# Attention's value product with its operands swapped, in a two-block transformer on one core

## The chip, the core and the metric

The kernel runs on one core of a Trainium2 chip. The metric is device time in microseconds for one execution of the whole program; three runs of the kernel before are shown below. Engines are named as in the profile: PE is TensorE (PEld its weight loads), DVE is VectorE, ACT is ScalarE, POOL is GpSimd, SP issues the transfers.

## What is computed

The reference takes 256 tokens of width 1024 through two layers of a first block (a gated feed-forward, a mixer of four kinds of attention, a second feed-forward) and one layer of a second block (a pooling mixer and two kinds of attention, gated and merged). All of it is float32. What matters here is the last step of each attention, the softmax weights times the values, row by row of queries:

```python
p = jax.nn.softmax(logits, axis=-1)
o = jnp.einsum('bhqk,bkhd->bqhd', p, v)      # 64 values wide for each head
```

The differential attention of the first block has two softmax maps per head, subtracted before the product with the values. The other kinds (neighbourhood, latent, grouped query; in the second block sliding window and one they call MoBA) have one map per head.

## The kernel before, in words

Activations stand by token: two token tiles of 128 rows. Projections are matmuls with 512 moving columns; each weight and each activation is held as a pair (hi, lo) of float32r numbers, so that one product is three matmuls into `mmps`. Weights come by transfers on SP's queue, 512 KB each, through a stage of three buffers. ScalarE makes the `hi` part and VectorE (every third one GpSimd) subtracts it to get `lo` (class `Weights`, lines 159 to 227); six places (`N_SPLIT`) hold the pairs.

Attention runs in the background of these projections. It is written as generators; after each group of matmuls `tick` (line 449) resumes up to four steps that are due. When a step is due is decided while the program is laid down, by the class `Clock` (from line 62) with estimated times for every operation. Only the order of issue rests on these estimates; what waits for what follows from the data. An operation of ScalarE or VectorE that reads PSUM is laid down with a priority that lets it pass 14 others (`AHEAD`, line 153).

`softmax_pv` (line 575) is the pipeline of one attention. A job is one token tile and two heads (`ns = 2`), or one differential head with its two maps (`ns = 1`). It has four steps: `scores` (line 584) computes the scores and the softmax weights `E` by query; `transposes` (line 631) transposes `E` on TensorE and has ScalarE copy it to `PT`, by key; `values` (line 641) multiplies; `finish` (line 660) puts the result, divided by the softmax sums, into `y` by query. The loop from line 674 chooses among the steps by `e_at`, `p_at` and `y_at`, the times at which `timed` (line 417) found a step's last operation off TensorE to end.

In `values` the values `v`, 128 keys by 64, are the stationary operand, and `PT`, 128 keys by 128 queries, is the moving one. The result is by value feature: 64 partitions for each head, the second head in the upper half. ScalarE copies it to `yt`; `finish` transposes that back on TensorE (line 338) and VectorE multiplies by `rs`. Two differential jobs fill the halves of one `yt` and share one transpose.

In the second block the first token tile sees one key tile (`nk = 1`), the second sees two; in the first block all jobs see two. The first block has 8 differential jobs and 12 two-head jobs in each of its two layers; the second block has 16 two-head jobs. The names in the trace: `PT` with `v`, `ug`, `vm` or `vs` are value products, `sps` are score tiles, `tps` is the ring of two PSUM tiles (`psT`, line 319) that transposes and value products share. Small fp32 matmuls stand in the trace as two matmuls each.

Of the kernel before, what the change touches and what calls it, by code (L numbers as in the profile page):

```python
# [10 lines left out]
F = mybir.dt.float32  # L11
R = mybir.dt.float32r
ACTF = mybir.ActivationFunctionType
ALU = mybir.AluOpType
# [47 lines left out]
class Clock:  # L62
    """Estimated times of the engines while the program is laid down. Only the order of issue
    rests on them; the waits themselves come from the data."""

# [34 lines left out]
    def ring(self, tag, bufs, ap):  # L100
        """A new tile of a ring takes the place of the one `bufs` before it."""
        r = self.rings.setdefault(tag, [])
        r.append(ap.tensor.name)
        if len(r) > bufs:
            old = r[-1 - bufs]
            t = max((e[2] for b in (self.writes, self.reads) for e in b.pop(old, ())),
                    default=0.0)
            self._note(self.reads, ap, t, "dma")
# [17 lines left out]
class Engine:  # L126
    """Passes calls on and keeps the engine's estimated time; what frees PSUM goes first."""

# [30 lines left out]
class Weights:  # L159
    """Weights in the order of their use: DRAM -> fp32 stage -> exact (hi, lo) float32r pair.  # L160
    Past the first units, which are waited for, GpSimd does every third subtraction."""

# [9 lines left out]
    def add(self, ap, k, n, per, cols=None):  # L172
        """ap [k*128, n] in DRAM, cut into units of `per` row tiles."""
        v = ap.rearrange("(k p) n -> p k n", p=128)
        if cols is not None:
            v = v[:, :, cols[0]:cols[1]]
            n = cols[1] - cols[0]
        k0 = 0
        for m in per if isinstance(per, list) else [per] * (k // per):
            assert m * n <= self.UNIT  # L180
            self.units.append((v[:, k0:k0 + m, :], m, n))
            k0 += m
        assert k0 == k
# [31 lines left out]
    def can_cut(self):  # L215
        """Whether the next unit's place is free of reads yet to be laid down."""
        n = len(self.cut_at)
        return bool(self.units or self.staged) and all(
            i in self.ended for i in range(max(0, n - N_SPLIT), n - N_SPLIT + 1))

    def get(self):
        """(index, hi, lo) of the next unit."""
        while not self.ready:
            self.cut()
        self.got += 1
        return (self.got - 1,) + self.ready.pop(0)
# [6 lines left out]
def decoder(ctx, tc, a, out):  # L233
# [4 lines left out]
    PSUM = bass.MemoryType.PSUM  # L238
# [26 lines left out]

# [1 line left out]
    for l in range(L):  # L267
# [32 lines left out]

# [1 line left out]
    def v3(ap, n):  # L302
# [39 lines left out]
    def acc(pss, xh, xl, w, j, first, last):  # L342
        """pss += x^T w with x = xh + xl, w = wh + wl; xl wl lies under float32's last bit."""
        _, wh, wl = w
        for ps, c0, n in pss:
            mm(ps, xh, wh[:, j, c0:c0 + n], first, False)
            mm(ps, xh, wl[:, j, c0:c0 + n], False, False)
        for ps, c0, n in pss:
            mm(ps, xl, wh[:, j, c0:c0 + n], False, last)

    def rpow(ss, n, inv, tag):
        """(ss * inv + eps) ** -0.5; several columns by a bitwise start and Newton steps."""
        m = stat.tile([128, n], F, tag=f"m{tag}{n}", name="ms")
        dve.tensor_scalar(m, ss, inv, EPS, op0=ALU.mult, op1=ALU.add)
        r = stat.tile([128, n], F, tag=f"r{tag}{n}", name="r")
        if n < 4:
            gps.tensor_tensor(out=r, in0=m, in1=mhalf[:, :n], op=ALU.pow)
            return r
        I = mybir.dt.int32
        dve.tensor_scalar(r.bitcast(I), m.bitcast(I), -0.5, float(0x5f3759df), op0=ALU.mult,  # L360
                          op1=ALU.add)
        q = stat.tile([128, 16], F, tag="q", name="q", bufs=1)[:, :n]
        for _ in range(3):
            dve.scalar_tensor_tensor(out=q, in0=m, scalar=-0.5, in1=r, op0=ALU.mult,
                                     op1=ALU.mult)
            dve.tensor_tensor(out=q, in0=q, in1=r, op=ALU.mult)
            dve.scalar_tensor_tensor(out=r, in0=q, scalar=1.5, in1=r, op0=ALU.add, op1=ALU.mult)
        return r
# [28 lines left out]
    def trans_split(hi, lo, src, scale=None):  # L397
        """src [128, 128 m] transposed and split into hi, lo [128, m, 128]."""
        ps = psT()
# [17 lines left out]
    def timed(f, *args):  # L417
        """f's result, and the time at which the last of its ops ends."""
        before, clock.last = clock.last, 0.0
# [36 lines left out]
    def drain_until(cond):  # L456
        """Background steps alone until cond holds; a step that is not due is brought forward."""
        while not cond():
# [9 lines left out]
    class Norm:  # L468
        """Residual update of one token tile, then the next projection's operand: x^T times the
        gains, which stand by feature in `gain`; the token's factor comes with the results."""  # L470

# [27 lines left out]
    def proj(K, n, per, evac, skew=False):  # L499
        """[256, 128 K] x [.., n <= 512]; evac(t, ps) takes each token tile's result."""  # L500
        ps = [psM() for _ in range(2)]
# [22 lines left out]
    def wide(order, hi, lo, blocks, evac, before=None):  # L524
        """[256, 128 len(order)] x [.., 1024]. A block of row tiles is done for token tile 0,
        then for token tile 1."""
        nk = len(order)
# [43 lines left out]

# [1 line left out]
    att = {"busy": False, "pt": 0}  # L573

    def softmax_pv(jobs, post, scored=None, have_v=lambda: True):
        """jobs: dict(t, nk, qk=[(lhsT, rhs)] * 2, bias=[ap] * 2 or None, v=[[ap] * nk] * 2, y).
        Two score tiles per job: two heads, or with `nlam` the two maps of a differential head;
        two such jobs share one value tile. Software pipeline: scores, transposes, values, out."""
        n = len(jobs)
        diff = "nlam" in jobs[0]  # L580
        ns = 1 if diff else 2
        E, PT, YT, yts = {}, {}, {}, {}

# [56 lines left out]

        def values(i):
            jb = jobs[i]
            ps = psT()[:, :128]
            for s in range(ns):
                r = slice(64 * s, 64 * s + 64)
                for k in range(jb["nk"]):
                    mm(ps[r, :], jb["v"][s][k], PT[i][:, s, k, :], k == 0, k == jb["nk"] - 1)
            if diff and i % 2 == 0:
                yts[0] = wk.tile([128, 128], F, tag="yt", name="yt")
            elif not diff:  # L650
                yts[0] = wk.tile([128, 128], F, tag="yt", name="yt")
            yt = YT[i] = yts[0]
            if diff:
                r = slice(64 * (i % 2), 64 * (i % 2) + 64)
                copy(0, yt[r, :], ps[0:64, :])
            else:
                copy(0, yt, ps)
            del PT[i]

        def finish(i):  # L660
            if diff and i % 2 == 0:
                return
            ps = psT()[:, :128]
            T(ps, YT[i])
            if diff:
                for j in (i - 1, i):
                    dve.tensor_scalar(jobs[j]["y"], ps[:, 64 * (j % 2):64 * (j % 2) + 64],
                                      jobs[j]["rs"][:, 0:1], None, op0=ALU.mult)
            else:
                dve.tensor_tensor(out=jobs[i]["y"], in0=heads(ps),  # L670
                                  in1=jobs[i]["rs"][:, :, None].to_broadcast([128, 2, 64]),
                                  op=ALU.mult)
# [42 lines left out]
    def mixers(l, cols, rows, nlam, norm_out):  # L715
# [76 lines left out]
        def qk_transposed(u, new, colq, colk, scale, hd, free=None):  # L792
            """Head norms and transposes of q (256) and k (256), split; both gains go on q."""
            qcol = stat.tile([128, 1], F, tag="qcol", name="qcol")
# [285 lines left out]

    # ================= block 1 =================
    gains = const.tile([128, 9, 8], F, name="gains")
# [41 lines left out]

    # ================= block 2 =================
    one = pool("one", 1)
# [28 lines left out]

    # MoBA: one block of 256 keys, so the selected slots are all masked
    def ev_cq(t, ps):
# [69 lines left out]
    def pooling():  # L1227
        """Windowed means less x, as a product with a constant band over the tokens."""
        pT = [v3(gates[1][:, t, 512:1024], 128) for t in range(2)]
# [215 lines left out]
```

## Time and profile before

| what | value |
|---|---|
| median of three runs | 1353.05 us (1350.02, 1353.05, 1357.2) |
| profiled execution, first to last instruction | 1349.9 us |
| instructions in the trace | 17823 |
| mean granted TensorE clock | 0.986 |
| moved by transfers | 221.80 MB, mean 164 GB/s |

The three runs are times of whole executions. The profile is of one execution, of which the span alone is given. A busy engine in the table of the page is one that has an instruction under way; matmuls are pipelined, so the distance between the starts of two of them says more of their price than the duration of one.

### The profile page before, as it was taken

How to read it: one execution, taken by the hardware profiler on the slowest of the kernel's cores; microseconds unless marked ns; L12 is line 12 of the kernel's file. 1: busy time of each engine (PE TensorE's matmuls, PEld its weight loads, DVE VectorE, ACT ScalarE, POOL GpSimd, SP SyncE). 2: the span in 40 equal slices, each digit the busy share in tenths (PEclk: the TensorE clock that was granted, in tenths of full speed). 3: DMA queues.
4: the chain of work that ended last, by engine and by line, in shares of the span. 5: the costliest groups of instructions: out<-in, count | busy, mean ns of one | idle time of the engine just before them, and what ended most of it. 6: DMA issues, size and time to landing. Idle time of an engine off the chain costs nothing.

```text
span 1349.9 us, 17823 instructions
## 1 busy us (share of the span) xinstructions
PE 1305.5 (97%) x6514; PEld 1055.0 (78%) x6514; DVE 700.6 (52%) x1488; ACT 722.9 (54%) x1223; POOL 330.8 (25%) x171
## 2 busy tenths in 40 slices
PE   8999999989999999999999998999999999999997
PEld 7788888766788888788888876788888776678876
DVE  5534338886543433644325798563442544544365
ACT  6544346756644443544435676665443456656543
POOL 0022223211222222322222321132222231122221
PEclk9999999989999999999999899999999999999999
DMA  8766547332466655566555633156656572345652
GB/s 273 213 187 188 176 149 235 112 102 64 134 203 177 197 174 170 179 203 189 179 186 166 202 108 97 45 184 193 185 184 187 174 225 80 103 130 168 212 160 78
DMA packets 109815, 221.80 MB, mean 164 GB/s; under 512 B 7456, under 2 KB 30368, under 8 KB 109728
## 3 DMA queue, kind: packets, MB, share of 16 engines
q1 hardware_dynamic: 109152, 220.04, 53.8%
q8 instruction: 51, 0.84, 0.3%
q10 hardware_dynamic: 576, 0.63, 0.1%
q14 instruction: 36, 0.29, 0.1%
HBM read 219.59 MB, written 1.05 MB: 163 GB/s over the span
## 4 chain that ended last, share of the span: by engine, by line
PE 79%; DVE 9%; DMA 5%; ACT 3%; issue 2%; POOL 1%; SPq 0%; POOLq 0%; ACTq 0%; DVEq 0%
PE mmps L336 67%; PE tps L340 6%; PE sps L336 3%; DVE lo L155 3%; PE tps L336 3%; DMA st<-in_w_in_dram 2%; DMA st<-in_ffn_w_gate_dram 2%; ACT hi L155 2%; DVE r L155 1%; DVE q L155 1%; DMA st<-in_ffn_w_up_dram 1%; DVE hss L155 1%; POOL lo L155 1%; DVE E L154 1%; ACT junk L155 0%
## 5 line engine op out<-in xcount | busy, mean ns | idle before, releaser
L155 ACT ACTIVATE hi<-st 128x1024 fp32r<-128x1024 f32 (+2 forms) x403 | 422.1, 1051 | 427.4 <-PE mmps L336 318.0
L155 DVE TENSOR_TENSOR lo<-st,hi 128x1024 fp32r<-128x1024 f32 (+2 forms) x276 | 350.1, 1271 | 474.8 <-ACT hi L155 474.3
L155 POOL TENSOR_TENSOR lo<-st,hi 128x1024 fp32r<-128x1024 f32 x127 | 304.7, 2399 | 813.7 <-ACT hi L155 746.6
L336 PE MATMUL mmps<-hi,xTh 128*128 128x512 f32 (+2 forms) x1200 | 458.0, 382 | 0.0
L336 PE MATMUL mmps<-hi,xTl 128*128 128x512 f32 (+2 forms) x1200 | 449.4, 375 | 0.2 <-DVE xTl L154 0.2
L336 PE MATMUL mmps<-lo,xTh 128*128 128x512 f32 (+2 forms) x1200 | 449.1, 375 | 0.0
L336 PEld LDWEIGHTS mmps<-hi,xTh 128*128 128x128 f32 x1200 | 229.0, 191 | 42.2 <-issue 4.5
L336 PEld LDWEIGHTS mmps<-hi,xTl 128*128 128x128 f32 x1200 | 228.9, 191 | 38.6 <-DVE xTl L154 0.6
L336 PEld LDWEIGHTS mmps<-lo,xTh 128*128 128x128 f32 x1200 | 229.0, 191 | 35.8 <-issue 0.5
L336 PE MATMUL mmps<-lo,hTh 128*128 128x512 f32 x352 | 139.9, 397 | 0.0
L336 PE MATMUL mmps<-hi,hTh 128*128 128x512 f32 x352 | 139.7, 397 | 0.0
L336 PE MATMUL mmps<-hi,hTl 128*128 128x512 f32 x352 | 116.0, 395 | 0.0
L336 PE MATMUL mmps<-hi,yT 128*128 128x512 f32 (+1 forms) x248 | 89.1, 416 | 0.0
L336 PEld LDWEIGHTS mmps<-hi,hTh 128*128 128x128 f32 x352 | 66.1, 188 | 15.8
L336 PEld LDWEIGHTS mmps<-hi,hTl 128*128 128x128 f32 x352 | 66.2, 188 | 15.5
L336 PEld LDWEIGHTS mmps<-lo,hTh 128*128 128x128 f32 x352 | 66.2, 188 | 15.0
L155 POOL TENSOR_TENSOR r<-ms,mhalf 128x1 f32<-128x1 f32 x40 | 26.1, 655 | 201.0 <-DVE ms L155 196.7
L336 PEld LDWEIGHTS mmps<-hi,yT 128*128 128x128 f32 x248 | 46.2, 191 | 11.2 <-issue 1.4
L336 PE MATMUL mmps<-lo,yT 128*128 128x512 f32 (+1 forms) x124 | 50.2, 405 | 0.0
L155 ACT ACTIVATE E<-E,nm 128x256 f32<-128x256 f32 (+1 forms) x80 | 38.2, 480 | 21.6 <-DVE nm L155 21.3
L154 ACT ACTIVATE xTh<-tps,gains 128x128 fp32r<-128x128 f32 x112 | 31.8, 374 | 23.8 <-PE tps L340 23.8
L154 DVE SCALAR_TENSOR_TENSOR fh<-mmps,r,fg 128x512 f32<-128x512 f32 (+1 forms) x48 | 32.6, 701 | 17.1 <-PE mmps L336 17.0
(173 smaller groups left out, 1099.5 us busy)
## 6 DMA issues: line engine op xcount, KB each, us to landing
st<-in_w_in_dram SPq DMA_DIRECT2D x90, 512.0 KB, 3.9
st<-in_ffn_w_up_dram SPq DMA_DIRECT2D x88, 512.0 KB, 4.4
st<-in_ffn_w_down_dram SPq DMA_DIRECT2D x88, 512.0 KB, 4.1
st<-in_ffn_w_gate_dram SPq DMA_DIRECT2D x87, 512.0 KB, 4.2
st<-in_w_out_dram SPq DMA_DIRECT2D x24, 512.0 KB, 3.6
st<-in_w_in_dram SPq DMA_DIRECT2D x8, 416.0 KB, 3.9
scratch<-in_t5b_dram SPq DMA_DIRECT2D x4, 512.0 KB, 5.3
scratch<-in_nab_dram SPq DMA_DIRECT2D x4, 512.0 KB, 7.3
```

Of the source, the lines that this page charges most:

```text
L154: return f(*args, **kw)
L155: return f(*args, **kw)
L336: nc.tensor.matmul(ps, lhsT=lhsT, rhs=rhs, start=start, stop=stop)
L340: nc.tensor.transpose(ps, src, ident)
```

## The change

`values` makes `PT` (128 keys by 128 queries) the stationary operand and `v` (64 columns) the moving one. The result is by query in one PSUM tile, 64 columns for each head, and stays there until `finish`, where VectorE multiplies it by `rs` into `y`. The copy to `yt` and the transpose are gone; each differential job now finishes by itself. The other lines of the diff only take away comments.

```diff
@@ softmax_pv
-        E, PT, YT, yts = {}, {}, {}, {}
+        E, PT, Y = {}, {}, {}
...
         def values(i):
             jb = jobs[i]
-            ps = psT()[:, :128]
+            Y[i] = psT()[:, :64 * ns]
             for s in range(ns):
-                r = slice(64 * s, 64 * s + 64)
                 for k in range(jb["nk"]):
-                    mm(ps[r, :], jb["v"][s][k], PT[i][:, s, k, :], k == 0, k == jb["nk"] - 1)
-            if diff and i % 2 == 0:
-                yts[0] = wk.tile([128, 128], F, tag="yt", name="yt")
-            elif not diff:
-                yts[0] = wk.tile([128, 128], F, tag="yt", name="yt")
-            yt = YT[i] = yts[0]
+                    mm(Y[i][:, 64 * s:64 * s + 64], PT[i][:, s, k, :], jb["v"][s][k], k == 0,
+                       k == jb["nk"] - 1)
+            del PT[i]
+
+        def finish(i):
+            ps, jb = Y.pop(i), jobs[i]
             if diff:
-                r = slice(64 * (i % 2), 64 * (i % 2) + 64)
-                copy(0, yt[r, :], ps[0:64, :])
+                dve.tensor_scalar(jb["y"], ps, jb["rs"][:, 0:1], None, op0=ALU.mult)
             else:
-                copy(0, yt, ps)
-            del PT[i]
-
-        def finish(i):
-            if diff and i % 2 == 0:
-                return
-            ps = psT()[:, :128]
-            T(ps, YT[i])
-            if diff:
-                for j in (i - 1, i):
-                    dve.tensor_scalar(jobs[j]["y"], ps[:, 64 * (j % 2):64 * (j % 2) + 64],
-                                      jobs[j]["rs"][:, 0:1], None, op0=ALU.mult)
-            else:
-                dve.tensor_tensor(out=jobs[i]["y"], in0=heads(ps),
-                                  in1=jobs[i]["rs"][:, :, None].to_broadcast([128, 2, 64]),
+                dve.tensor_tensor(out=jb["y"], in0=heads(ps),
+                                  in1=jb["rs"][:, :, None].to_broadcast([128, 2, 64]),
                                   op=ALU.mult)
```

## Rows read from the trace of the kernel before

**Rows 1.** The page's first two parts: span, busy time of each engine.
```profile
span 1349.9 us, 17823 instructions
PE 1305.5 (97%) x6514; PEld 1055.0 (78%) x6514; DVE 700.6 (52%) x1488; ACT 722.9 (54%) x1223; POOL 330.8 (25%) x171
```

**Rows 2.** The page's chain that ended last, share of the span by engine.
```profile
PE 79%; DVE 9%; DMA 5%; ACT 3%; issue 2%; POOL 1%; SPq 0%; POOLq 0%; ACTq 0%; DVEq 0%
```

**Rows 3.** Windows: stretch, length, busy PE, PEld, DVE, ACT, POOL, clock, DMA, GB/s.
```profile
228.00:276.00 48.00, 43.23 (x244) 33.59 (x244) 39.38 (x139) 35.46 (x85) 11.43 (x7) 0.93 0.44 124
...
1085.00:1190.00 105.00, 100.84 (x567) 72.98 (x566) 50.96 (x159) 60.39 (x145) 17.02 (x8) 0.98 0.42 126
```

**Rows 4.** Tile PT: durations min/median/max in ns, first and last start, forms.
```profile
L336 PE MATMUL tps<-PT,v x192: 272/273/477, 244.3 to 856.7; 128*64 128x128 f32 x192
...
L336 PE MATMUL tps<-PT,ug x64: 272/273/324, 333.9 to 870.5; 128*64 128x128 f32 x64
...
L336 PE MATMUL tps<-PT,vm x48: 272/273/477, 1118.6 to 1145.0; 128*64 128x128 f32 x48
```

**Rows 5.** Tile yt: the copy and the transpose back, columns as above.
```profile
L154 ACT ACTIVATE yt<-tps x56: 254/277/280, 245.0 to 1189.4; 128x128 f32<-128x128 f32 x40, 64x128 f32<-64x128 f32 x16
...
L340 PE MATMUL tps<-ident,yt x48: 270/272/473, 248.6 to 1189.8; 128*128 128x128 f32 x48
```

**Rows 6.** Timeline of PE, a differential block: start us, us, instruction.
```profile
246.93 0.40 PE L336 MATMUL mmps<-hi,yT 128*128 128x512 f32 x1
247.26 0.65 PE L336 MATMUL tps<-PT,v 128*64 128x128 f32 x4
247.84 0.50 PE L336 MATMUL mmps<-hi,xTh 128*128 128x512 f32 x1
248.17 0.39 PE L336 MATMUL mmps<-lo,xTh 128*128 128x512 f32 x1
248.40 0.39 PE L336 MATMUL mmps<-hi,xTl 128*128 128x512 f32 x1
```

**Rows 7.** Timeline of PE, a two-head block with two key tiles.
```profile
341.57 0.39 PE L336 MATMUL mmps<-hi,yT 128*128 128x512 f32 x1
341.89 0.67 PE L336 MATMUL tps<-PT,ug 128*64 128x128 f32 x8
...
342.83 0.40 PE L336 MATMUL mmps<-lo,yT 128*128 128x512 f32 x1
```

**Rows 8.** Timeline of PE, a two-head block with one key tile.
```profile
1156.67 0.40 PE L336 MATMUL mmps<-hi,xTl 128*128 128x512 f32 x1
1156.99 0.44 PE L336 MATMUL tps<-PT,vs 128*64 128x128 f32 x4
...
1157.70 0.40 PE L336 MATMUL mmps<-lo,xTh 128*128 128x512 f32 x1
```

**Rows 9.** Timeline of PE, a differential block next to scores.
```profile
244.31 0.65 PE L336 MATMUL tps<-PT,v 128*64 128x128 f32 x4
244.89 0.63 PE L336 MATMUL sps<-qkT 32*128 32x256 f32 x6
```

**Rows 10.** Timeline of PEld, weight loads of the pooling product.
```profile
1173.76 0.97 PEld L336 LDWEIGHTS tps<-band,gate 128*128 128x128 f32 x8
```

**Rows 11.** Timeline of PE, four transposes in a row.
```profile
275.49 0.60 PE L340 MATMUL tps<-ident,qe 128*96 128x128 f32 x4
```

**Rows 12.** Tile y: multiplications; then, of VectorE's idle us and times before it, the first.
```profile
L154 DVE TENSOR_TENSOR y<-tps,rs x40: 270/291/293, 305.3 to 1190.1; 128x128 f32<-128x128 f32 x40
...
  PE tps L340: 21.4, 24
```

**Rows 13.** Timeline of all engines, 270 to 281 us.
```profile
274.71 2.40 POOL L155 TENSOR_TENSOR lo<-st,hi 128x1024 fp32r<-128x1024 f32 x1 [7.11 <-ACT hi L155]
...
274.79 2.35 DVE L155 TENSOR_SCALAR ms<-hss 128x8 f32<-128x8 f32 x1
...
279.94 0.66 PE L340 MATMUL tps<-ident,yn 128*128 128x128 f32 x2 [3.38 <-DVE q L155]
```

## The prediction, made before the changed kernel was run

> **What bounds the kernel now.** I read the page's busy times first. TensorE is busy for 97% of a span of 1349.9 us [rows 1], so time can only be won where TensorE is given less to do or is kept from waiting. The page's chain of the work that ended last says the same: 79% of it is TensorE, 9% VectorE, 3% ScalarE [rows 2]. A share over the whole span hides the stages, so I looked next at the stretches in which the value products lie. In the first layer's attention stretch, 228 to 276 us, TensorE is busy 43.2 of 48 us and VectorE 39.4; in the second block's, 1085 to 1190 us, 100.8 of 105 us against 51.0 for VectorE and 60.4 for ScalarE [rows 3]. So the second block's attention is TensorE's almost alone, and the first layer's is shared: what TensorE gains there is partly handed to VectorE's chain. The profiled execution is the span of 1349.9 us; nothing is shown of what lies around it. It agrees with the lowest of the three runs (1350.0) and lies 3.15 us under their median, so I work out a difference on the profiled span and apply it to the median.
>
> **How much work the change touches.** The trace has 192 value matmuls from `v`, 64 from `ug` and 48 from `vm` [rows 4], and 48 more from `vs` with the same durations: 352 pairs of a weight load and a matmul, two pairs for each matmul of the program. They come in 56 blocks, one per job: 16 differential jobs (one head, two key tiles, 4 pairs), 32 two-head jobs with two key tiles (8 pairs) and 8 two-head jobs of the second block with one key tile (4 pairs). 16 x 4 + 32 x 8 + 8 x 4 is 352. Today a block is followed by a ScalarE copy of 277 ns, 56 in all, and by a transpose back, 48 in all because two differential jobs share one [rows 5]. Copies and transposes go. VectorE's multiplications by `rs`, 56 of them, stay, of the same size; only their source becomes the value product itself.
>
> **What a block costs TensorE today.** I measure a block by how late the second big matmul after it starts. Ordinary 512-column matmuls start 0.23 to 0.235 us apart (248.17 to 248.40). A differential block stands between 246.93 and 248.17: 1.24 less two ordinary pitches of 0.235 is 0.77 us [rows 6]. A two-head block with two key tiles stands between 341.57 and 342.83: 1.26 less 0.47 is 0.79 us for twice the pairs [rows 7]. With one key tile it is 1157.70 less 1156.67 less 0.47, so 0.56 us [rows 8]. Read together: 8 pairs cost as much as 4 because the two heads' 64-column halves run side by side; a step of one pair per half costs (0.79 - 0.56) / 2, some 0.11 us; and each block carries a fixed 0.34 us (0.77 - 4 x 0.11, 0.56 - 2 x 0.11) in which the array goes from whole to half use and back, with the first loads uncovered. Where a score block stands next to a value block, part of that fixed cost is the score block's in any case: the differential block at 244.31 is followed by scores at 244.89, 0.58 us later [rows 9].
>
> **What a block will cost.** A weight load becomes 128 columns and the moving operand 64, and the array stays whole. The trace has such loads in the pooling product, 128 columns fp32 with 128 moving: 8 loads take 0.97 us from first to last, and with 0.19 for the last alone that is 0.78 / 7, some 0.11 us a pair, with no gap to the work before or after [rows 10]. Whether halving the moving columns shortens a pair is not shown. From below: 0.055 us, if the moving columns set the 0.11. From above: 0.16 us, the load's 0.11 and half of it again for 64 columns not hidden behind the next load. I take 0.11, the row it is nearest to, since the load has the same 128 columns. Then a differential block costs 0.45 us, a two-head block 0.89, a one-key-tile block 0.45.
>
> **The sum, TensorE's side.**
> - Differential: some 10 blocks stand alone and win 0.77 - 0.45 = 0.32 us, 6 beside scores win 0.58 - 0.45 = 0.13 us: +4.0 us.
> - Two heads, two key tiles: 32 x (0.79 - 0.89) = -3.2 us. Here the change costs.
> - Two heads, one key tile: 0.56 - 0.45 = 0.11 us for the half that stand alone, about nothing beside scores: +0.4 us.
> - Transposes back: four transposes in a row take 0.60 us, less 0.27 for the last, over three steps, so 0.11 us each [rows 11]; 48 x 0.11 = +5.3 us.
>
> That makes 6.5 us. The differential part of it, 4.0 and 8 transposes of 0.11, lies in stretches where VectorE is often what is late, so I take 2 us off. I add 1 us for the ends of the chains: the last value product of a token tile, then copy, transpose, multiplication, normalisation. That chain becomes shorter by 277 ns, 272 ns and two handovers, but TensorE mostly has other work meanwhile. The sum is 5.5 us: 1344.4 on the profiled span, **1347.5 us** against the median.
>
> **What I cost at nothing.** The 56 ScalarE copies (15.5 us) lie beside TensorE's work; ScalarE is busy 54% of the span [rows 1]. If ScalarE were the late one, they would be worth up to their 15.5 us. PSUM: the ring `tps` has two places. A job took three, now two, so the next transposes wait for less; but the value tile is now held until VectorE has multiplied it rather than until ScalarE has copied it. VectorE's multiplication (291 ns) is itself no longer or shorter; it waited 21.4 us in 24 waits for the transpose [rows 12], and will wait for the value product instead. What stands behind it on VectorE is the weights' subtractions, and these have six places of slack. No DMA and no instruction of SP's or POOL's queue is added or moved. In the plan, `values` has no operation off TensorE, so `timed` gives 0 for it and `finish` is due at the very next step; a program order is laid down with other estimates (128 moving columns are planned at 216 ns a matmul, 64 at 110 ns), so all orders around attention shift.
>
> That shift is the uncertainty. VectorE's small operations take 2.35 us where one meets GpSimd's subtraction of 2.40 us, and one such meeting at 274.79 is followed by a wait of 3.38 us of TensorE at the transpose of `yn` [rows 13]. Two or three such meetings more or fewer on the chain are 5 us either way.
>
> **The rivals.**
> - *More than the sum*: the meetings fall better, or ScalarE's relief and the shorter chains tell, or a pair is nearer to 0.055. Half of the extra gain of that last (352 x 0.055 = 19 us) would not show, since VectorE's chain is next. For it: VectorE and ScalarE waits in the first layers' attention. Some 5 us more: 1342 us.
> - *The gain goes into new waits*: VectorE stands at a multiplication whose value product is still to run, and the score rows and subtractions behind it come late. 56 multiplications of which each may wait a block of up to 0.89 us; it eats the 5.5 us when a fifth of that total of 50 us reaches TensorE. Against it: VectorE is busy 52%, and it waits there today. 1353 us.
> - *Slower, the loads uncovered*: with only 64 columns moving, a load of 128 does not hide, and a pair costs 0.16 us. Place: all 56 blocks. Price: 352 x 0.05 = 17.6 us more, so 1365 us. It decides from 0.11 + 5.5 / 352 = 0.126 us a pair, and is slower by over 0.5% from 0.146. Against it: the pooling loads, each 0.11 us after the one before it.
> - *Slower, the halves were worth it*: if the fixed 0.34 us stays in a block of whole-array pairs (because it is the wait for the weights `PT`), only the steps count: 32 x (0.44 - 0.88) - 8 x (0.44 - 0.22) + 5.3 = -10.6 us, so 1364 us. Against it: the pooling loads have no such cost.
>
> On that last rival the Trainium skill's page "TensorEngine Tiling (Array Packing)", section "When to Use Tiling", speaks against this change: for a moving operand of at most 64 columns it advises to swap the operands and use two column tiles, which is the kernel before. By that rule alone the time would be the 1364 us of this rival. The same page's "Key Properties" says that a change of tiling mode drains the engine, and the fixed 0.34 us of a block agrees with that.
>
> **How the numbers follow.** A measurement of this kernel tells about 0.5% (6.8 us) from no change. The forecast, 1343 to 1352 us, has 0.58; more than the sum 0.17; new waits 0.15; loads uncovered 0.06; halves worth it 0.04. Faster by over 0.5% means under 1346.3: all of the second case and 0.23 of the forecast, 0.40. Slower: the last two and 0.01 of the waits, 0.11. Within: 0.49. The range leaves out the two slow rivals and the far end of the second case: 1340 to 1356 us.
>
> **What would show it.** Right: value matmuls as 128*128 with 64 moving columns, their loads 0.11 us apart and no gap around the block; `yt` gone; two-head blocks at 0.89 us and differential ones at 0.45. Wrong: loads 0.16 apart; a block still 0.34 us over its pairs; VectorE's wait at `y` well over 21.4 us with TensorE waiting on VectorE behind it; or a different count of 2.3 us operations on VectorE, which would say that the time came from their luck and not from the blocks.

## The result, and the profile of the changed kernel

The changed kernel is **slower by 0.7%**: 1356.84 us median of 8 runs (1353.7 to 1364.32) against 1349.3 us of 8 runs of the kernel before on the same chip (1344.61 to 1357.2), ratio 1.007, 95% interval 1.005 to 1.009. The forecast was 1347.5 us and the range ended at 1356. The profiled execution took 1362.46 us, its span 1360.3: some 2.1 us lie around the span. This execution lies 5.6 us above the median. With the same 2.1 us around it, the span of before, 1349.9, belongs to an execution of some 1352 us (an estimate), 2.7 above its median and not the 1350.0 that the prediction took it for. So the two profiles are further apart (10.4 us) than the medians (7.5). The forecast also counted from the median of three runs, 1353.05; from the 1349.3 of eight, its saving of 5.5 us would give 1343.8.

First the page of the changed kernel, its first two parts and the chain that ended last (against [rows 1, 2]):

```profile
span 1360.3 us, 17679 instructions
PE 1308.6 (96%) x6466; PEld 1076.3 (79%) x6466; DVE 697.4 (51%) x1488; ACT 713.0 (52%) x1167; POOL 331.8 (24%) x171
...
PE 76%; DVE 10%; DMA 5%; issue 4%; ACT 4%; POOL 1%; SPq 0%; POOLq 0%; ACTq 0%; DVEq 0%
```

TensorE has 48 matmuls less, and yet is busy for 3 us longer; the span is 10.4 us longer, so some 7 us are new idle time, and VectorE, ScalarE and issue have a larger share of the chain.

**Were the prices right?** The products by operand and form (answering to [rows 4]), then two blocks of the second block's attention, one with one key tile and one with two, on TensorE's timeline (to [rows 7, 8]):

```profile
L336 PE MATMUL tps<-v,PT x192: 217/275/422, 242.8 to 873.1; 128*128 128x64 f32 x192
```

```profile
1178.45 0.39 PE L336 MATMUL mmps<-hi,xTl 128*128 128x512 f32 x1
1178.68 0.55 PE L336 MATMUL tps<-vs,PT 128*128 128x64 f32 x4
...
1179.36 0.39 PE L336 MATMUL mmps<-lo,xTh 128*128 128x512 f32 x1
...
1193.53 0.39 PE L336 MATMUL mmps<-hi,xTl 128*128 128x512 f32 x1
1193.76 1.00 PE L336 MATMUL tps<-vs,PT 128*128 128x64 f32 x8
...
1194.89 0.39 PE L336 MATMUL mmps<-lo,xTh 128*128 128x512 f32 x1
```

By the prediction's measure, four pairs cost 1179.36 - 1178.45 - 0.47 = 0.44 us, and eight cost 1194.89 - 1193.53 - 0.47 = 0.89. Forecast were 0.45 and 0.89. The copy to `yt` and the transpose of it [rows 5] are gone. So the two slow rivals about the pairs (loads uncovered, halves worth it) did not come about; the time was lost elsewhere.

**Where it was lost.** I cut both executions some 0.2 us before the last matmul of each feed-forward's second product starts: a stretch from the first feed-forward of a layer to its second one (attention, output projection, feed-forward), twice, and the second block. The columns are stretch, length, TensorE busy and its matmuls, granted clock, transfer share, GB/s. The kernel before:

```profile
201.40:540.80 339.40, 328.65 (x1696) 0.97 0.52 156
...
733.80:1069.10 335.30, 326.29 (x1696) 0.98 0.51 155
1069.10:1319.40 250.30, 242.60 (x1202) 0.99 0.51 156
```

The changed kernel:

```profile
200.40:547.50 347.10, 331.02 (x1680) 0.97 0.51 152
...
741.50:1087.30 345.80, 331.20 (x1680) 0.96 0.50 150
1087.30:1329.80 242.50, 237.41 (x1186) 0.99 0.53 161
```

The two layers lose 7.7 and 10.5 us, and the second block gains 7.8. Of the layers' 18.2 us, 10.9 are idle time of TensorE (length less busy: 19.8 us before, 30.7 after), the rest is busy time. That rest is not more work. At a granted clock of 0.50, which is 1.2 GHz, TensorE was busy for 47.1 us of these stretches, against 24.8 before. If half of such time is what the lower clock costs (its big matmuls are 0.43 us apart there instead of 0.23, shown below), the clock accounts for some 11 us, and at full clock the work would have become some 4 us shorter; both are estimates. So idle time and the lower clock each made about 11 us, and the lesser work gave 4 back. In the narrow stretches of [rows 3] next to nothing of it is seen; in the first of them TensorE is even a little busier:

```profile
228.00:276.00 48.00, 43.86 (x242) 35.93 (x242) 39.64 (x139) 34.89 (x80) 13.05 (x7) 0.93 0.49 140
1085.00:1190.00 105.00, 100.69 (x549) 79.45 (x548) 58.76 (x172) 65.02 (x143) 23.99 (x12) 0.98 0.51 153
```

**The place.** The longest waits of TensorE in the changed kernel (engine, operation, what it waited for; total, times, longest):

```profile
PE tps L340 <- DVE y L154: 9.5, 2, 4.9
PE sps L336 <- ACT E L154: 8.1, 6, 3.4
```

Neither stood in the list of before, where the first was 5.7 us behind VectorE's `q`. The 9.5 us at `y` are one place, once in each layer. All engines of the changed kernel there:

```profile
278.80 0.55 PE L336 MATMUL tps<-v,PT 128*128 128x64 f32 x4
...
279.51 0.61 PE L336 MATMUL sps<-qkT 32*128 32x256 f32 x5
279.57 1.22 DVE L155 TENSOR_TENSOR lo<-st,hi 128x1024 fp32r<-128x1024 f32 x1
...
281.11 2.34 POOL L155 TENSOR_TENSOR lo<-st,hi 128x1024 fp32r<-128x1024 f32 x1 [6.61 <-ACT hi L155]
281.45 2.02 DVE L155 SCALAR_TENSOR_TENSOR r<-q,r 128x8 f32<-128x8 f32 x1
...
284.11 0.69 DVE L155 TENSOR_TENSOR u<-u,r 128x512 f32<-128x512 f32 x1
284.72 0.28 DVE L154 TENSOR_SCALAR y<-tps,rs 128x64 f32<-128x64 f32 x1
...
285.05 0.69 PE L340 MATMUL tps<-ident,E 128*128 128x128 f32 x2 [4.93 <-DVE y L154]
```

The value product is done at about 279.3. Its multiplication stands on VectorE behind a subtraction, the norms of another mixer (`q`, `r`, `u`), and one of these small operations stretched to 2.02 us beside GpSimd's subtraction. The multiplication starts at 284.72. Until then the value product holds one of the two places of `tps`; the transposes at 285.05 wait for `y`, and TensorE stands for 4.93 us. The stretched operation makes some 1.85 us of that (2.02 less the 0.17 of others of its shape); the rest is the queue that stands before the multiplication. The granted clock around it:

```profile
279.50:284.70 5.20, 0.62 (x6) 1.00 0.59 195
284.70:291.50 6.80, 6.45 (x21) 0.50 0.22 74
291.50:296.00 4.50, 4.50 (x30) 1.00 0.01 4
```

After 5.2 us in which TensorE was busy for 0.62, it runs the next 6.8 us at 0.50, which is 1.2 GHz. Its matmuls of 512 columns are 0.43 us apart there instead of 0.23, and the four pairs that start at 288.48 give way to the next group after 0.74 us, those at 1178.68 after 0.37.

The longest wait for `E` is another VectorE queue of the same kind:

```profile
300.38 0.42 DVE L154 TENSOR_REDUCE nm<-sps 128x1 f32<-128x256 f32 x1
...
300.89 0.47 ACT L154 ACTIVATE E<-sps,nm 128x256 f32<-128x256 f32 x1 [2.17 <-DVE q L155]
...
301.51 1.88 PE L336 MATMUL sps<-kT,qT 96*128 96x256 f32 x4 [3.42 <-ACT E L154]
```

The row maximum `nm` comes late behind norms of other mixers, ScalarE's `E` behind it, and the score tiles behind that. From 301.76 to 312.00 the granted clock is 0.50 again.

This is what the changed kernel looked like at its worst place. Whether the held place is the cause, or only where a late VectorE is seen, the profile alone does not say.

### The profile page after: what moved, and what is told of

It is laid out like the page before. It is cut to its first block, busy times and chain, and to the rows that moved or that the text cites. A ratio compares the mean times of both kernels' runs of the same rounds, so it can differ in the third digit from the quotient of the medians.

```text
span 1360.3 us, 17679 instructions
## 1 busy us (share of the span) xinstructions
PE 1308.6 (96%) x6466; PEld 1076.3 (79%) x6466; DVE 697.4 (51%) x1488; ACT 713.0 (52%) x1167; POOL 331.8 (24%) x171
## 4 chain that ended last, share of the span: by engine, by line
PE 76%; DVE 10%; DMA 5%; issue 4%; ACT 4%; POOL 1%; SPq 0%; POOLq 0%; ACTq 0%; DVEq 0%
PE mmps L336 67%; PE tps L340 4%; DVE lo L155 3%; PE tps L336 3%; DMA st<-in_w_in_dram 2%; PE sps L336 2%; ACT hi L155 2%; DMA st<-in_ffn_w_gate_dram 1%; DVE r L155 1%; DMA st<-in_ffn_w_up_dram 1%; DVE q L155 1%; POOL lo L155 1%; DVE E L154 1%; POOL r L155 1%; DVE nm L155 1%
## 5 line engine op out<-in xcount | busy, mean ns | idle before, releaser
L154 ACT ACTIVATE PT<-tps 128x512 f32<-128x512 f32 (+1 forms) x56 | 28.1, 502 | 43.1 <-PE tps L340 42.5
L340 PE MATMUL tps<-ident,E 128*128 128x128 f32 x176 | 34.0, 302 | 14.7 <-DVE y L154 9.5
```

The lines of the kernel that those rows point to most:

```text
L154: return f(*args, **kw)
L340: nc.tensor.transpose(ps, src, ident)
```

## The experiments

One table for all of them. "Layers" is the length of the two layers' stretches together, "idle" the part of it in which TensorE was not busy, "second" the second block's stretch, each from one profiled execution cut as above; the ratio is of medians, to the kernel before as measured beside each run, with its interval. The stretches are good to some 3 us: runs 5, 6 and 15 have, in the layers, the very order of issue of before, changed and run 9, and differ from them by 2.7, 2.1 and 3.2 us. The profile of run 1 also lies 7.5 us under its median, that of run 16 6.9 under, that of run 2 4.3 above.

| kernel | ratio | layers us | idle us | second us |
|---|---|---|---|---|
| before | 1 | 674.7 | 19.8 | 250.3 |
| changed | 1.007 (1.005 to 1.009) | 692.9 | 30.7 | 242.5 |
| 1 operands swapped, copy and transpose kept | 1.0143 (1.0118 to 1.0167) | 682.5 | 23.7 | 249.8 |
| 2 copy kept, transpose gone | 1.003 (1.0015 to 1.0045) | 682.2 | 21.8 | 248.1 |
| 3 ScalarE multiplies | 1.0042 (1.0026 to 1.0058) | 684.6 | 27.4 | 241.6 |
| 4 `finish` due when the product ends | 1.0027 (1.0011 to 1.0043) | 680.1 | 25.7 | 242.2 |
| 5 second block alone changed | **0.994 (0.9917 to 0.9962)** | 672.0 | 19.2 | 241.9 |
| 6 layers alone changed | 1.0111 (1.0062 to 1.0161) | 690.8 | 27.9 | 248.7 |
| 7 before, another order | 1.0043 (1.0019 to 1.0067) | 675.5 | 23.5 | 250.2 |
| 8 changed, another order | 1.0148 (1.0107 to 1.019) | 699.4 | 26.1 | 241.2 |
| 9 changed, planned as before | 0.9987 (0.9969 to 1.0005) | 672.4 | 19.9 | 245.1 |
| 10 differential jobs and second block | 1.0145 (1.0115 to 1.0175) | 696.2 | 31.6 | 241.7 |
| 11 two-head jobs alone | 1.0029 (1.0002 to 1.0056) | 683.1 | 21.9 | 242.2 |
| 12 ScalarE multiplies, due when it ends | 1.0041 (1.0018 to 1.0064) | 679.1 | 29.1 | 247.7 |
| 13 plan's price mended | 1.0046 (1.0029 to 1.0064) | 680.1 | 25.4 | 248.3 |
| 14 price and due time mended | 1.0022 (1.0002 to 1.0041) | 686.1 | 26.4 | 240.6 |
| 15 layers planned as before | 0.9974 (0.9962 to 0.9987) | 675.6 | 23.2 | 241.6 |
| 16 due 253 ns later | 1.0164 (1.0134 to 1.0194) | 693.6 | 31.6 | 241.8 |
| 17 third place still counted | 1.0012 (0.9993 to 1.003) | 672.0 | 20.0 | 246.8 |

The first theory was that the held place costs the layers; its rivals were the swap itself, and the order of issue.

**1 and 2, the swap apart from what it takes away.** In the first, the kernel before with

```diff
-                    mm(ps[r, :], jb["v"][s][k], PT[i][:, s, k, :], k == 0, k == jb["nk"] - 1)
+                    nc.tensor.matmul(ps[:, r], lhsT=PT[i][:, s, k, :], rhs=jb["v"][s][k],
+                                     start=k == 0, stop=k == jb["nk"] - 1)
```

and all else kept, so that the result is in another layout. In the second, ScalarE copies the swapped product to `yt` by query, VectorE multiplies from there, and the transpose back is gone. The second charges the plan what the kernel before charged. The first does so for the products; but its copies of the differential jobs now have 64 columns instead of 128, for which the plan charges 54 ns less each, so that its order of issue is another one too.

> The kernel before with the operands of the value product swapped and nothing else: the copy and the transpose back stay, so the attention results come out in another layout than the reference's. Issue order stays near that of before. By the block prices (differential +4.0 us, two heads with two key tiles -3.2, one key tile +0.4) it is 0 to 2 us faster than before, ratio 0.998 to 1.000. Theory 'the swap itself is dear' (some price of the swapped product that the blocks do not show): 7 us or more slower, ratio 1.005 or more. Theory 'new waits come with the value tile held for VectorE': they are not in this kernel, so near 1.000.

> Operands swapped, transpose back gone, but ScalarE still copies the value tile out of PSUM at once, and VectorE multiplies from the copy. The estimates of the planner are those of before. Theory 'the value tile held for VectorE makes the score transposes wait': the wait of the transposes of E for y (9.5 us in 2 waits in the changed kernel) is gone, and the time is 3 to 7 us under before, ratio 0.995 to 0.998. Rival 'a shifted issue order of any kind costs it': ratio 1.00 to 1.01 with waits in other places.

The first took 1366.89 us, the second 1353.25, against 1347.95. The first lies where its expectation put a dear swap, 1.4% slower. But its order differs from that of before, ScalarE loads its activation tables 11 times instead of 9, and its profile shows only 7.8 us more in the layers; so it does not part the swap from the order, and why it is the slower one stays open. Against a dear swap speaks run 9 below, which has it in every job. With ScalarE freeing the place at once, the second's idle time in the layers is near that of before (21.8 us) and no wait for `y` is left. That is what the held place asks for; but the time lies where the rival, a shifted order of any kind, had put it, and the layers are still 7.5 us longer (in an execution 4.3 us over the median), so it wasn't all.

**3 and 4, two remedies in the changed kernel.** ScalarE does the multiplication (`scaled(...)` for each head); or the due time counts the value product:

```diff
-                y_at[i3] = timed(values, i3)
+                y_at[i3] = max(timed(values, i3), clock.pe + clock.LAG["pe"])
```

> The changed kernel with the multiplication by rs done by ScalarE out of PSUM (one operation per head) in place of VectorE. Theory 'VectorE is behind at this point and holds the value tile': the wait for y of the score transposes goes, ratio to before 0.993 to 0.999. Rival 'it is the order': ratio 1.003 to 1.010 as the changed kernel. Rival 'the swap itself': 1.005 or more.

> The changed kernel with one line of the planner changed: the step that multiplies by rs is due when the value product is planned to end, not at once. Theory 'laid down too early, the multiplication blocks VectorE in front of the product': VectorE's wait for the value product (32.5 us in 36 waits) shrinks and the time comes down, ratio to before 0.995 to 1.000. Theory 'held value tile': later multiplication holds the tile longer, so no better than the changed kernel, ratio 1.005 to 1.012.

1353.09 and 1351.42 us against 1347.95: the first where the rival "it is the order" had put it, the second between its two cases. Each takes back part of the layers' loss, and in each another wait of TensorE appears: 9.6 us in two waits for `yT` in the first, 5.7 in two for `qT` in the second.

**5 and 6, the two halves of the program.** The kernel before, with the changed `values` and `finish` only where

```diff
+        if jobs[0]["nk"] == 1:
+            values, finish = values_q, finish_q
```

which is the second block, and in the other kernel `== 2`, the layers.

> The swap in the second block alone (16 jobs); the two layers are as before, with the same issue order. In the changed kernel the second block's stretch, from the last product of the second layer to the end, took 265.6 us against 273.4. Theory 'the loss lies in the layers only, the second block gains': layers as before, second block 7 to 9 us shorter, ratio 0.992 to 0.996, faster than both kernels. Rival 'the gain there was a chance of how that execution met the layers' end': ratio 0.998 to 1.002.

> The swap in the two layers alone (40 jobs); the second block is as before, and the layers have the changed kernel's issue order. Theory 'the loss lies in the layers only': 14 to 20 us slower than before, ratio 1.010 to 1.015, slower than the changed kernel. Rival 'loss is spread or chance': ratio 1.004 to 1.008 as the changed kernel.

1341.2 us and 1364.75 against 1348.73. The gain and the loss are separate and add up: -0.6% and +1.1%, together +0.5, against +0.7 measured for both. The second block alone changed beats both kernels. Between medians the layers lose 16.0 us and the second block gains 7.5.

**7 and 8, other orders of the same instructions.** `AHEAD` (how many instructions a PSUM read may pass) 16 instead of 14, in the kernel before and in the changed one. Nothing else differs.

> A control without the change: the kernel before with AHEAD 16 in place of 14, so that operations that read PSUM may pass two more others. The same instructions, another issue order. Theory 'issue order alone moves this kernel by about as much as the change did': ratio differs from 1 by 0.003 or more to the slow side, since 14 was picked for this program: 1.003 to 1.012. Rival 'order is worth nothing, the change's loss has a price of its own': 0.998 to 1.002.

> The changed kernel with AHEAD 16 in place of 14: the same instructions, another issue order. Theory 'order decides': the two waits of the layers (score transposes for y, scores for E) move or go, and the ratio to before lies somewhere in 0.995 to 1.012, off the changed kernel's 1.007 by 0.003 or more. Rival 'the loss has a price of its own': 1.006 to 1.008.

1354.9 us and 1368.75 against 1348.73: the order alone is worth 0.4% in the one and 0.8% (1.0148 against 1.007) in the other. A difference of the size in question can come from the order. In run 8 no wait of TensorE for `y` is left, and its layers are the longest of the table: 71.7 us of them ran at 0.50, against 51.2 in the changed kernel.

**9, the changed instructions in an order planned as before.** `values` and `finish` tell `Clock` of a copy, a transpose back with its place in `tps`, and matmuls of 128 columns that the program no longer has:

```diff
+                    clock.op("pe", 128 / 2.4 * 4 + 3, [ps[:, :128]], [v, p])
...
+            clock.op("act", 55 + 0.84 * 128, [yts[0]], [ps[:, :128]])
...
+                clock.ring("t", 2, pt)
+                clock.op("pe", 110, [pt], [yt])
```

> The changed kernel's instructions, but the order is planned as if copy, transposes back and 128 moving columns were still there. It differs from the kernel that kept the copy (ratio 1.003, its two layers 682 us together) in one thing of substance: the value tile stays in tps until VectorE has multiplied. If the held place is what costs the layers, they come to about 690 us again and the time to 1357 or more, TensorE waiting over 4 us at a transpose for y. If the due time in the plan was at fault, the layers come to about 680 and the time to 1346 to 1350.

1345.97 us against 1348.5. Its page counts the same instructions as the changed kernel's, 6466 matmuls, 1488 and 1167 operations of VectorE and ScalarE; their order is neither that of the changed kernel nor quite that of before. Its stretches, cut in the same way:

```profile
201.40:537.50 336.10, 326.94 (x1680) 0.97 0.51 157
...
731.40:1067.70 336.30, 325.55 (x1679) 0.98 0.50 155
1067.70:1312.80 245.10, 236.64 (x1185) 1.00 0.51 159
```

The layers take 672.4 us instead of 692.9, less than the 680 of the better of the two cases, and the value tile is still held until VectorE has multiplied it. What TensorE waits for at `y` (line 659 is the swapped product, 687 the multiplication):

```profile
PE tps L659 <- DVE y L687: 2.8, 2, 2.0
```

2.8 us instead of 9.5. At the same place of the program, the same norms and a stretched operation are there, but two multiplications come ahead of `u` and of the next subtraction (278.67 and 280.09):

```profile
275.04 2.34 DVE L155 TENSOR_TENSOR q<-q,r 128x8 f32<-128x8 f32 x1
...
277.38 0.27 DVE L687 TENSOR_SCALAR y<-tps,rs 128x64 f32<-128x64 f32 x1
...
277.70 0.66 PE L659 MATMUL tps<-v,PT 128*128 128x64 f32 x4 [0.72 <-DVE y L687]
...
278.40 0.28 DVE L687 TENSOR_SCALAR y<-tps,rs 128x64 f32<-128x64 f32 x1
```

So the theory of the held place falls: holding it costs next to nothing in another order, in run 8 the layers are slow without any wait for `y`, and in run 13 below TensorE waits for it for 8.0 us in layers of 680.1. The order of issue is the cause. How much the hold adds within the changed kernel's own order was not tried: each run that gives the place back sooner has another order too.

**10 and 11, which jobs.** The condition becomes `diff or jobs[0]["nk"] == 1`, and in the other kernel `not diff`.

> Swapped in the 16 differential jobs and in the second block; the 24 two-head jobs of the layers as before. The second block alone swapped gave 1341.2. The first of the new waits stands behind the last differential job (4.9 us, and the same place in layer 2, with a clock of 1.2 GHz behind it). If the held place at the differential jobs is the cause, most of the layers' 16 to 18 us is here: 1352 to 1358. If the two-head jobs are (dearer blocks, late scores), this is as good as 1341 or better by the 4 us of the differential blocks: 1337 to 1343.

> The complement: all two-head jobs swapped, those of the layers and of the second block; the differential jobs as before. If the differential jobs carry the layers' loss: 1340 to 1345 (the block prices alone say 2.4 us more for 24 jobs and 2.6 us less for their transposes). If the two-head jobs carry it: 1353 to 1358.

1368.51 us and 1352.55 against 1348.5. With the differential jobs changed the layers take 24.2 us more than in run 5 (696.2 against 672.0), with the two-head jobs 11.1. TensorE waits 6.4 us for `y` and 8.2 us for `E` in the one, for neither over 2 us in the other. Neither forecast was met: the first is 10 us beyond the dearer of its cases, the second half a microsecond short of the dearer of its own. Most of the loss enters with the differential jobs, whose steps stand among the norms of other mixers in the rows above, but the two-head jobs have a part too, and the two do not add up (35 us against 20.9 for both at once). Order is shared between them, so no sum over jobs tells it.

**12, both remedies.**

> The changed kernel with both remedies: ScalarE multiplies by rs, and finish is due when the value product ends. Alone they gave 1353.1 (ratio 1.0042) and 1351.4 (1.0027). If they mend two different things, the layers come to about 670 us and the time to 1340 to 1344. If each only moves the same late VectorE chain to another instruction, this stays at 1348 to 1354.

1353.29 us, no better than either alone, as the second case had it: the lateness moves to another instruction (idle is 29.1 us here).

**13, 14, 16 and 17, which entry of the plan.** In the first, `mm` charges `max(_free(rhs), 128)` columns; in the second, that and the due time of run 4; in the third, another `+ 253` in that due time; in the fourth, instead of it, `clock.ring` and the transpose's `clock.op` in `finish`.

> The changed kernel, but the plan charges a matmul of 64 fp32 columns like one of 128 (216 ns instead of 110), nearer to the two pairs of 0.11 us that it takes. finish is still due at once. If the price is at fault, the layers fall from 693 to about 675 us and the time to 1341 to 1347. If the due time is, it stays at 1353 to 1360.

> Both mended: the price of 64 columns and finish due when the value product ends. If the two together are what was wrong with the plan, this comes to the time of the plan of before or under it, 1339 to 1346. If it stays near the 1351 of the due time alone, what helps in the plan of before is something else: the third tps place that it still counts for each job, or chance.

> As with price and due time mended (1350.8), but finish due another 253 ns later: the 163 ns that the plan charged for the copy and its 90 ns of handover. If it is the lateness that keeps the multiplication out of VectorE's queue until its value product is there, this comes to 1344 to 1347. If not, it stays at 1349 to 1352.

> As with price and due time mended (1350.8), and the plan still counts the third place of tps and the transpose of 110 ns at finish, which the program no longer has. If it is the spacing of the jobs that this gives, 1344 to 1347; if not, 1349 to 1352.

1354.5, 1350.78, 1368.78 and 1348.76 us against some 1348. The price alone leaves the time where the due time's being at fault would leave it; in its profile it takes 12.8 us off the layers and puts 5.8 on the second block. Price and due time together stay near the due time alone. The third place on top of them takes the layers to 672.0 us, as good as before, and the time to between its two cases. Of the later due time both cases failed: these instructions, due a quarter of a microsecond later, are 1.6% slower than the kernel before (and, as in run 1, the order makes ScalarE load its tables 11 times). No entry by itself mends it, and the time does not go one way with any of them. What is shown is that the order decides; a rule for a good order is not.

**15, the best of the changed code.** All products swapped, layers planned as in run 9, second block by the changed code's plan.

> All value products swapped; the layers planned as before, the second block by the changed code's own plan. The layers gave 672.5 us together in the first, the second block 265 us in the second, against 268.2 planned as before: 1346.0 less 3 is 1343. If the second block's plan depends on where the layers end, no gain: 1346.

1345.04 us against 1348.31, ratio 0.9974: between its two cases, 0.3% faster than before, not as fast as run 5.

**Why the second block gains 8 us.** On TensorE's timeline, two stretches of the kernel before. The first has no transpose back in it; in the second, one stands ahead of the same groups of scores and transposes of `E`, which are left out here:

```profile
1181.22 0.40 PE L336 MATMUL mmps<-hi,xTl 128*128 128x512 f32 x1
1181.54 0.70 PE L336 MATMUL sps<-kT,qT 64*128 64x256 f32 x2
1182.17 0.66 PE L340 MATMUL tps<-ident,E 128*128 128x128 f32 x4
1182.76 0.70 PE L336 MATMUL sps<-kT,qT 64*128 64x256 f32 x2
...
1183.73 0.40 PE L336 MATMUL mmps<-lo,xTh 128*128 128x512 f32 x1
```

```profile
1127.45 0.39 PE L336 MATMUL mmps<-hi,xTl 128*128 128x512 f32 x1
1127.68 0.27 PE L340 MATMUL tps<-ident,yt 128*128 128x128 f32 x1
...
1130.06 0.40 PE L336 MATMUL mmps<-lo,xTh 128*128 128x512 f32 x1
```

and the same work in run 5:

```profile
1157.95 0.39 PE L336 MATMUL mmps<-hi,xTl 128*128 128x512 f32 x1
1158.27 0.70 PE L336 MATMUL sps<-kT,qT 64*128 64x256 f32 x4
1158.91 0.66 PE L340 MATMUL tps<-ident,E 128*128 128x128 f32 x4
...
1159.63 0.40 PE L336 MATMUL mmps<-lo,xTh 128*128 128x512 f32 x1
```

From the big matmul before it to the second one after it, the first takes 2.51 us, the second 2.61, the third 1.68. So the transpose back is 0.10 us, as forecast. The other 0.83 is that the two score tiles, which use 64 rows of the array, are parted by the transposes of `E`, which use 128, so that the array goes to half rows and back twice. Scores parted by other products occur 6 times in the second block before and twice in run 5, which makes some 3.3 us.

Whether scores are parted is a matter of order, not of the transpose back: the first stretch has none, and run 17, which has no transpose back at all, parts its scores 6 times as before and takes 246.8 us there. The runs that part them once or twice took 240.6 to 242.5 us, those that do it three or four times 242.2 to 248.3, five or six times 246.8 to 250.3. The 8.4 us of run 5 are 6.9 us of busy time (242.6 to 235.7) and 1.5 of idle time (7.7 to 6.2). To the busy time belong 16 transposes of 0.11 and the 3.3 us; some 3 us more are the clock (an estimate: before, TensorE was busy for 6.3 us at 0.50 there, in run 5 for none). These sum to a little more than is measured, and no run separates them.

## Why the prediction was wrong

**The prices: right.** A pair at 0.11 us, blocks of 0.45 and 0.89, no fixed cost left: measured 0.44 and 0.89. A differential block next to scores took 1.15 us with them where it was 1.33. In the order planned as before (run 9) the layers gain 2.3 us; the sum gave them 4.0 - 2.4 + 3.5 = 5.1, less 2 for VectorE's being late, so 3.1. The 2.3 agree with that but are no more than two executions of one order differ by.

**The second block: right in sign, short in size.** The sum gave it 1.4 us (16 transposes of 0.11, the one-key blocks' 0.4, less 0.8); run 5 measured 8.4. The transpose back was priced rightly, 0.11 us by a row of transposes [rows 11] and 0.10 as a lone one. What the sum has no term for is the order again: scores parted twice instead of 6 times, and less time at the lower clock.

**The step that failed** is "What I cost at nothing", in its last part: "all orders around attention shift", and "two or three such meetings more or fewer on the chain are 5 us either way". The shift was seen, and the place too [rows 13]; its size was not, nor what sets it. The same instructions in other orders took from 0.9974 to 1.0164 of the time before (changed, 4, 8, 9 and 13 to 17 differ in order alone, but for two table loads more in 16), about 25 us from end to end, and the order that the changed code plans for itself cost the layers 16.0 us by the medians of run 6, 18.2 in the profile. The number of meetings is not its measure: VectorE operations on at most 16 columns that took over 1 us are 11 in the layers before and 12 in the changed kernel, 23.7 and 24.2 us in all, and 10 both in the slow run 16 and in the good run 15. So the different count that the prediction named as a sign did not come. What changed is which operations stand in VectorE's queue before those that TensorE needs, and the longest waits of TensorE were followed by stretches at 1.2 GHz, which the sum did not have.

**The held place** was named and costed at nothing, and run 9, which holds it too, bears that out for its order. It is where lateness shows; that it makes none in the changed kernel's own order is not shown.

**The rivals.** "The gain goes into new waits" had the direction, at 0.15 and 1353 us, and of the waits one: score rows came late, as the 8.1 us for `E` show. (The 5.5 us that it eats are a ninth of its 50, not a fifth.) But VectorE's standing at a multiplication was not what cost. VectorE's wait for the value product did grow, from 21.4 us in 24 waits [rows 12] to

```profile
  PE tps L336: 32.5, 36
...
  PE tps L340: 9.5, 2
```

(the first row is VectorE's idle time before `y`, the second who waited for `y`). In run 9 it grew to 29.3 us, and no time was lost; what costs is TensorE standing for VectorE, at `y` as in the second row or at `E`. "More than the sum" holds for the second block alone. "Halves worth it" named a time, 1364 us, that was not far off, for a reason that was not there: its nearness is luck. The Trainium skill's "TensorEngine Tiling (Array Packing)", "When to Use Tiling", would have kept the halves; by the measured blocks its advice is worth 0.10 us on a two-head block and costs 0.3 us on a differential one, and run 9, with whole-array products throughout, has no loss. The same page of the Trainium skill says under "Key Properties" that a change of tiling mode drains the engine; the 0.83 us that parted scores cost agree with that.

**The range** should have let the order alone move the kernel by over 1% either way. A planner whose estimates change with the edit was in the code; one constant of the order, changed in the kernel before and nothing else, moved that by 0.4% (run 7).

## What to carry to other kernels

Where the order of issue comes from estimates, an edit that changes an estimate is two edits: keep the plan of before under the new instructions once, and only then judge the instructions (here 1.007 became 0.9987). Apply a change stage by stage: the same edit gained 0.6% in the stage that TensorE bounds alone and lost 1.1% in the stage it shares with a late VectorE. And look at what the order puts between two products of one shape: two score tiles with transposes between them took 0.83 us more than side by side, while the lone transpose back that was taken away was worth 0.10.

## What was not expected of the hardware

Two score tiles parted by transposes cost 0.83 us more than side by side (64-row against 128-row products, 2.51 against 1.68 us). A wait of 4.93 us in TensorE was followed by 6.8 us at a granted clock of 0.50, one of 3.42 us by 10.2, and the changed kernel has more of that: some 51 us at 1.2 GHz in the two layers' stretches against 27 before. The clock is a large part of the loss there, but not the whole of it in every order: of the six executions of run 16, the slowest took 1371.34 us at a mean clock of 0.979 and the fastest 1357.42 at 0.991, where executions of the kernel before at 0.991 took 1346.47 to 1349.06.
